# The squares of five pre-norms added to one pair of tiles on VectorE, so that TensorE sums two tiles instead of five

## The chip, the cores and the metric

The kernel runs on one core of one Trainium2 chip. The metric is the device time of one launch in microseconds (us), as the median of three runs. The times are compared kernel against kernel; the profile is of one further execution.

## The reference, cut to what matters

Two stacks of two layers each are applied to x of 256 tokens and 1024 channels, all in float32. Each layer of the first stack ("first block") is a pre-norm, a mixing part with three branches, an output projection with a norm of its own ("post-norm"), a sum with x, then the same around a feed-forward part. Each layer of the second stack ("second block") has a pre-norm before the mixing part and one before the feed-forward part. All these norms are root-mean-square norms over the 1024 channels:

```
xn = x * rsqrt(mean(x * x, channels) + eps) * g      # eps = 1e-6
```

With two layers a block there are eight such pre-norms: four in the first block and four in the second.

## The kernel before, in words

Channels lie on the 128 partitions, so that x is eight tiles of 128 channels by 256 tokens (`KD` = 8, `T` = 256), and the mean over channels is a sum over tiles and partitions. A column of sums over partitions is made on TensorE, by a product with a matrix of ones in plain float32 (`sumsq`, L599).

Nearly all of the work is products of weights and activations. Each float32 factor is split into two float32r parts (`hi`, `lo`), and a product is three float32r products. The weights come as a stream of 512 KB chunks of eight 128x128 blocks: a load to `wraw`, a rounding on ScalarE to `whi`, a subtraction on VectorE to `wlo` (`Weights.ensure`, L311; four buffers each). A chunk feeds 24 products of 256 columns. After four of the norms the first chunk of each of the first two products goes to TensorE as plain float32, against the tile `yw`.

The first two products after a pre-norm take x before it is scaled per token (tiles `yh`, `yl`), and their results are scaled on the way out of the accumulator (`dfr`). So the scale `r` of a token is needed only when those two products are done. By the third product, `whole` (L676) must have made the scaled x as `hh` and `hl`.

`post_norm` (L736) is where this change acts in four cases. It takes the unscaled result `zg` of an output projection and makes u = s * x + zg by pairs of tiles on VectorE; for each pair `feed` (L651) writes `yh` on ScalarE and `yl` on VectorE, and then sends the pair to `sumsq`: a square on ScalarE into a tile `sqt` (three buffers, one of which `yw` holds for a time), and an addition to the first pair's tile on VectorE, for as many pairs as `last` allows. At `last` the two halves of the sum are added too ("the fold"), and the result and the later tiles go to TensorE one by one. `end_norm` (L662) makes `r` from the sum in two steps on VectorE, with a square root on ScalarE and a reciprocal on VectorE.

`start_norm` (L640) sets `last` by its argument `folded`, which is 4 unless the caller says otherwise. Callers that say nothing are `run` (the first pre-norm, whose x is just being loaded) and `post_norm` (four pre-norms). `residual` (L1057) passes 6 for the three other pre-norms that have sums in their own products. `out_proj` (L774) calls `start_sum` itself with 6 and `hold`.

The order on each engine is fixed when the program is built: a planner simulates the program with costs of its own, takes the instructions in the order in which the program wrote them unless one isn't ready by its simulation, and so writes a queue for each engine. `issue_after` and `urgent` tie some instructions to come behind others; the weights after a norm of a feed-forward part have a higher priority (`W.first`). Steps of work beside the products (branches, attention) are woven in by `side` (L475), which keeps two counters, `pe` and `dve`, of estimated ns, and holds such steps back while `dve` is over `pe + SLACK` (4000).

Of the kernel before, what the change touches and what calls it, by code (L numbers as in the profile page):

```python
# [46 lines left out]
# norms after which the first chunks of weights and what they meet go unsplit  # L47
WHOLE = (1, 2, 3, 4)
# tiles of a product that ends a chain, the last ones apart
COLUMNS = ((0, 2), (2, 2), (4, 2), (6, 1), (7, 1))  # L50
# gates and products of the branches, in their order
# [8 lines left out]
def ffn_up(arr, l):  # L60
    """Gate and value tiles side by side; the first two products take four tiles."""
    t = [[_cols(i * P, P), _cols(FF + i * P, P)] for i in range(KF)]
    return [(arr, (l,), "B", KD, c) for c in [t[0] + t[1], t[2] + t[3]] + t[4:]]


def plan():
    """The weights in the order in which the tensor engine takes them: (array, index, kind,
    k tiles, columns), kind "B" by column tiles of 128 and "A" by rows of 512."""
    jobs = []

    def seg(arr, idx, nk, off, n, step=256):
        for i in range(0, n, step):
            jobs.append((arr, idx, "B", nk, [_cols(off + i + j, P) for j in range(0, step, P)]))

    def last_singly(arr, idx, nk):
        seg(arr, idx, nk, 0, D - 256)
        seg(arr, idx, nk, D - 256, 256, P)

    for l in range(DEPTH):
        seg("w_in", (l,), KD, OFF1["cfb"], 512, 512)  # L80
        seg("w_in", (l,), KD, OFF1["cfa"], 512, 512)
        for s, n in (("q", 256), ("k", 256)):
            seg("w_in", (l,), KD, OFF1[s], n)
        jobs.append(("w_in", (l,), "A", KD, _cols(OFF1["v"], 512)))
        for s, n in (("scc", 512), ("scx", 512), ("scb", 512), ("g", 512)):
            seg("w_in", (l,), KD, OFF1[s], n)
        for what, b in BRANCHES1:
            if what == "g":
                seg("w_in", (l,), KD, OFF1["gate"] + b * D, D)
            else:  # L90
                seg(("w_ret_out", "w_sc_out", "w_cf_out")[b], (l,), 4, 0, D)
        last_singly("w_o", (l,), KD)
        jobs += ffn_up("w_up", l)
        last_singly("w_down", (l,), KF)
    for l in range(DEPTH):
        w = "w_in_2"
        misc = np.full(P, -1)
        misc[:64] = _cols(OFF2["ik"], 64)
        misc[64:72] = _cols(OFF2["mif"], 8)
        misc[72:76] = _cols(OFF2["iw"], 4)  # L100
        jobs.append((w, (l,), "B", KD, [_cols(OFF2[s] + j, P) for s in ("iq", "ckv") for j in (0, P)]))
        seg(w, (l,), KD, OFF2["mqk"], 512, 512)
        jobs.append((w, (l,), "B", KD, [misc]))
        seg(w, (l,), KD, OFF2["mqk"] + 512, 512)
        jobs.append((w, (l,), "A", KD, _cols(OFF2["mv"], 512)))
        seg(w, (l,), KD, OFF2["mo"], 512)
        seg(w, (l,), KD, OFF2["dq"], 512)
        seg(w, (l,), KD, OFF2["dk"], 512)
        jobs.append((w, (l,), "A", KD, _cols(OFF2["dv"], 512)))
        seg("dsa_w_kv_up_2", (l,), 2, 0, 512)  # L110
        jobs.append(("dsa_w_kv_up_2", (l,), "A", 2, _cols(512, 512)))
        seg(w, (l,), KD, OFF2["sq"], 512)
        for what, b in BRANCHES2:
            if what == "g":
                seg(w, (l,), KD, OFF2["gate"] + b * D, D)
            else:
                seg("w_branch_2", (l, b), 4, 0, D)
        seg("w_out_2", (l,), KD, 0, D)
        jobs += ffn_up("w_gate_up_2", l)
        if l + 1 < DEPTH:  # L120
            seg("w_down_2", (l,), KF, 0, D)
        else:
            last_singly("w_down_2", (l,), KF)
    return jobs
# [48 lines left out]
def pack_params(inputs=None):  # L173
    """Per-channel parameters, channels on partitions: (offsets, array)."""
# [38 lines left out]
def make_consts():  # L213
    """Tables that depend on shapes alone: (offsets, array [128, n])."""
# [56 lines left out]
def whole_chunks():  # L271
    """The chunks that go to the tensor engine as float32, unsplit."""
    out, n, i = set(), 0, 0
    for _, _, kind, nk, cols in plan():
        if kind == "B" and len(cols) == 4:
            if i // 2 in WHOLE:
                out.add(n // CB)
            i += 1
        n += nk * (len(cols) if kind == "B" else 4)
    return out  # L280


class Weights:
    """The stream of weights: loads ahead, then each chunk as the sum of two float32r parts."""
# [13 lines left out]
    def cuts(self, c):  # L298
        """The first chunk comes in halves."""
        return [slice(0, CW // 2), slice(CW // 2, CW)] if c == 0 else [slice(0, CW)]  # L300
# [43 lines left out]
class Gen:  # L344
# [102 lines left out]
    def split(self, hi, lo, src):  # L447
        """src as the sum of its float32r rounding and of the exact rest."""
# [3 lines left out]
    def behind(self, engine):  # L452
        """What is traced here is issued after the engine's last urgent instruction."""
# [21 lines left out]
    def side(self):  # L475
        """Steps of the tasks beside the products, as far as the vector engine keeps up."""
# [13 lines left out]
    def job(self, evac, mov, needs=(), scale=None, last=False, spare=None):  # L490
        """The next product of the plan. mov(k) gives the two parts of the activations' tile k;
        scale, per token, is for activations that were not normalised yet; spare gives tiles."""
# [3 lines left out]
        if kind == "B":  # L496
            n = len(cols)
            accs = [self.acc() for _ in range(-(-n // 2))]
            if self.idle is not None:
                # only to keep the tensor engine's clock up while it waits  # L500
# [4 lines left out]
            for k in range(nk):  # L505
                xs = mov(k)
                for t in range(n):
# [4 lines left out]
                    # a start clears the marks of its whole bank: the first product of a bank has it  # L512
# [32 lines left out]
    def swap(self, out, src):  # L545
        """src with the halves of each 64 channels exchanged"""
# [3 lines left out]
    def rows(self, r):  # L550
        # r in DRAM, from where a row goes to many partitions
# [4 lines left out]
    def spread(self, out, row):  # L556
        """a row on all the partitions of out"""
        self.nc.sync.dma_start(out, row.to_broadcast(list(out.shape)))

# [31 lines left out]
    def rstd(self, pool, ps, scale, name):  # L591
        """1 / sqrt(scale * ps + eps)"""
# [6 lines left out]
    def sumsq(self, out, last, hold):  # L599
        """Over channels, on every partition: the sum of the squares of the eight tiles, which it  # L600
        takes by pairs, the last two also one by one (send). The first ones are added up before.
        With hold the tensor engine gets them together at the end."""
        ps = self.sp()[:, :T]
        n, todo = 0, []
        while n < KD:
# [14 lines left out]
            if n == last:  # L620
# [19 lines left out]
    def start_norm(self, g, l, folded=4):  # L640
        """Takes x by pairs of tiles (feed) for a norm whose scale per token comes last."""
# [20 lines left out]
    def end_norm(self, sd=None):  # L662
        """What the first products take, with their scale, and what the others take."""
# [38 lines left out]
    def branches(self, order, bufs, pool, mov, gate_load, needs, ys, done):  # L702
        """The sum over branches of gate * (branch output times its matrix), as two parts. A gate
        sigmoid(z) comes as tanh(z / 2), its double less 1."""
# [31 lines left out]
    def post_norm(self, zg, sums, gpre, l):  # L736
        """x += normalised zg; then the next norm's input. With s the root mean square of z, what
        the norm sees is u = s * x + zg, s times the new x."""
# [23 lines left out]
    def unscale(self, sd):  # L762
        """x out of u"""
# [10 lines left out]
    def out_proj(self, mov, g, l):  # L774
        """Four products whose columns are scaled by g, with the sum of their squares."""
# [11 lines left out]
    def first_mix(self, l, norm):  # L787
        dmov, rs, whole, mov = norm
        nc = self.nc
        with ExitStack() as st:  # L790
# [6 lines left out]
            def new_y(b):  # L797
                """Buffers for a branch's output, once those of the one before last are free."""
# [13 lines left out]
            # conformer convolution  # L812
# [65 lines left out]
            # retention  # L878
# [44 lines left out]
            # short convolution  # L923
# [133 lines left out]
    def residual(self, mov, gpre, l):  # L1057
        """x += four products; then the next norm's input."""
# [17 lines left out]
    def second_mix(self, l, norm):  # L1076
        dmov, rs, whole, mov = norm
        nc = self.nc
        with ExitStack() as st:
# [11 lines left out]
            def new_y(b):  # L1091
                """Buffers for a branch's output, once those of the one before last are free."""
# [14 lines left out]
            def rope(o):  # L1107
                """Rotates two tiles in place."""
# [6 lines left out]
            # indexer  # L1115
# [63 lines left out]
            # key/value rank  # L1179
# [33 lines left out]
            def q_task(sqs, dst, rq):  # L1213
                """rotation of the queries, and their scale per token and head"""
# [39 lines left out]
            # mLSTM queries and keys  # L1254
# [29 lines left out]
            # mLSTM gates  # L1284
# [102 lines left out]
            # attention with a softmax: sets of (queries, keys) of 64 channels  # L1387
            def softmax_group(q, k, rq, t, grp, bias, p, sums):
                """p = exp(scores - max) for the queries of tile t, sums its row sums. A group is
                sets in the same half of the partitions, one a tile."""  # L1390
# [22 lines left out]
            def transposed(p):  # L1413
                """p by keys: for each set its blocks of keys"""
# [18 lines left out]
            def ahead(q, k, rq, t, bias):  # L1433
                """The groups of tile t with their softmax, one group ahead."""
# [49 lines left out]
            def diff(l=l):  # L1484
                init = 0.8 - 0.6 * math.exp(-0.3 * l)
                for t in range(2):
                    yt = tl([P, 512], "yt", tag="yt", bufs=3)
                    for (half, tiles), p, sums in ahead(dq, dk, rq_d, t, None):
# [5 lines left out]
                        # both maps in one, up to the first one's sums  # L1494
# [44 lines left out]
            # differential attention  # L1539
# [22 lines left out]
            # sparse attention: keys and values out of the rank  # L1562
# [72 lines left out]
```

## Time and profile before

| what | value |
|---|---|
| time, median of 3 runs | 1789.97 us (1788.31 to 1790.07) |
| profiled execution: span from first to last instruction | 1789.1 us |
| TensorE busy | 1777.4 us of the span (99%) |
| VectorE busy | 1363.0 us (76%) |
| ScalarE busy | 1111.0 us (62%) |

For the profiled execution the page gives the span alone, and no time around it; the span is 0.9 us under the median of the runs. Busy time is the share in which an instruction of that engine was under way. Matmuls overlap each other, so the distance between their starts says more than the duration of one. A plain float32 product of 256 columns stands in the trace as two records, a float32r product as one.

### The profile page before, as it was taken

The page shows a single profiled execution, that of the slowest core. Times are in us where ns is not written, and L with a number is a line of the kernel's source. Part 1 is how long each engine was busy: PE and PEld are TensorE (multiplying, and loading weights), DVE is VectorE, ACT ScalarE, POOL GpSimd, SP SyncE. Part 2 cuts the span into 40 slices and gives each one's busy share as a digit, 9 for nine tenths or more (in the row PEclk, how much of TensorE's full clock was granted, in tenths as well). Part 3 has the DMA queues.
Part 4 walks back from the last instruction along what each step waited for, and adds up shares of the span by engine and source line. Part 5 has one row for each costly group of instructions (what it writes and reads, how often), then busy time and mean ns, then how long its engine had stood idle before and what let it go on. Part 6 is the DMA issues. An engine that isn't in the chain of part 4 may idle for free.

```text
span 1789.1 us, 35765 instructions
## 1 busy us (share of the span) xinstructions
PE 1777.4 (99%) x14462; PEld 1729.2 (97%) x14462; DVE 1363.0 (76%) x2082; ACT 1111.0 (62%) x1787; POOL 70.2 (4%) x144
## 2 busy tenths in 40 slices
PE   8999999999999999999999999999999999999999
PEld 8999999999999999999998999999999999999999
DVE  8988679865999769884887877865569887677553
ACT  7575468755666567765576666654457666655542
POOL 0000000000000000000022100000000310000000
PEclk9999999999999999999999999999999999999999
DMA  7555546554655546555465644565555664356663
GB/s 265 191 171 179 187 154 200 188 187 164 210 168 188 177 138 204 189 189 188 137 195 177 201 142 139 168 207 194 189 186 180 199 201 139 124 177 200 193 196 132
DMA packets 94648, 322.52 MB, mean 180 GB/s; under 512 B 12257, under 2 KB 16913, under 8 KB 94482
## 3 DMA queue, kind: packets, MB, share of 16 engines
q1 hardware_dynamic: 91010, 314.15, 53.9%
q0 software_dynamic: 3328, 6.09, 1.1%
q8 instruction: 113, 1.85, 0.4%
q14 instruction: 53, 0.43, 0.1%
q10 hardware_dynamic: 144, 0.00, 0.0%
HBM read 312.80 MB, written 1.10 MB: 175 GB/s over the span
## 4 chain that ended last, share of the span: by engine, by line
PE 97%; DVE 1%; DMA 1%; issue 0%; ACT 0%; POOL 0%; SPq 0%; DVEq 0%; ACTq 0%; POOLq 0%
PE acc L403 90%; PE sp L403 6%; PE sp L408 1%; DMA tmp<-dq 0%; DMA Wm<-rows 0%; DMA x<-x 0%; DVE wlo L415 0%; DVE sc L1167 0%; DVE x L415 0%; DVE m L1166 0%; DVE yw L420 0%; ACT sd L445 0%; DVE dq L415 0%; ACT whi L326 0%; POOL tmp L548 0%
## 5 line engine op out<-in xcount | busy, mean ns | idle before, releaser
L326 ACT ACTIVATE whi<-wraw 128x1024 fp32r<-128x1024 f32 (+1 forms) x575 | 606.7, 1057 | 535.9 <-PE acc L403 367.8
L415 DVE TENSOR_TENSOR wlo<-wraw,whi 128x1024 fp32r<-128x1024 f32 (+1 forms) x575 | 699.0, 1220 | 282.9 <-ACT whi L326 281.3
L403 PE MATMUL acc<-hh,whi 128*128 128x256 f32 x2832 | 791.4, 280 | 0.0
L403 PE MATMUL acc<-hl,whi 128*128 128x256 f32 x2832 | 790.8, 280 | 0.0
L403 PE MATMUL acc<-hh,wlo 128*128 128x256 f32 x2832 | 789.9, 280 | 0.0
L403 PEld LDWEIGHTS acc<-hh,whi 128*128 128x128 f32 x2832 | 531.0, 188 | 5.5 <-issue 3.7
L403 PEld LDWEIGHTS acc<-hl,whi 128*128 128x128 f32 x2832 | 531.7, 188 | 1.9 <-issue 1.2
L403 PEld LDWEIGHTS acc<-hh,wlo 128*128 128x128 f32 x2832 | 531.4, 188 | 1.1 <-issue 0.8
L403 PE MATMUL acc<-yh,whi 128*128 128x256 f32 x1280 | 269.7, 284 | 6.2 <-ACT whi L326 6.2
L403 PE MATMUL acc<-yh,wlo 128*128 128x256 f32 x832 | 231.3, 283 | 0.0
L403 PEld LDWEIGHTS acc<-yh,whi 128*128 128x128 f32 x1280 | 210.5, 190 | 7.1 <-ACT whi L326 6.2
L403 PE MATMUL acc<-fh,wlo 128*128 128x256 f32 x704 | 196.0, 278 | 0.0
L403 PE MATMUL acc<-fl,whi 128*128 128x256 f32 x704 | 195.6, 278 | 0.0
L403 PE MATMUL acc<-fh,whi 128*128 128x256 f32 x704 | 195.5, 278 | 0.0
L403 PEld LDWEIGHTS acc<-yh,wlo 128*128 128x128 f32 x832 | 155.8, 189 | 0.4
L403 PEld LDWEIGHTS acc<-fh,wlo 128*128 128x128 f32 x704 | 132.3, 188 | 0.0
L403 PEld LDWEIGHTS acc<-fl,whi 128*128 128x128 f32 x704 | 132.2, 188 | 0.0
L403 PEld LDWEIGHTS acc<-fh,whi 128*128 128x128 f32 x704 | 132.0, 188 | 0.0
L403 PE MATMUL acc<-yl,whi 128*128 128x256 f32 x384 | 108.2, 282 | 0.0
L403 PEld LDWEIGHTS acc<-yl,whi 128*128 128x128 f32 x384 | 72.1, 188 | 0.2
L445 ACT ACT_TABLE_LOAD x50 | 64.2, 1283 | 5.5 <-DVE Wm L426 3.0
L420 DVE SCALAR_TENSOR_TENSOR up<-z,prm,up 128x254 f32<-128x254 f32 (+1 forms) x128 | 55.3, 479 | 0.0
(282 smaller groups left out, 1815.2 us busy)
## 6 DMA issues: line engine op xcount, KB each, us to landing
wraw<-stream SPq DMA_DIRECT2D x581, 512.0 KB, 3.6
kr<-rows SPq DMA_DIRECT2D x32, 64.0 KB, 3.0
dec<-decay SPq DMA_DIRECT2D x2, 768.0 KB, 4.3
x<-x SPq DMA_DIRECT2D x4, 256.0 KB, 6.3
rf<-rows SPq DMA_DIRECT2D x8, 128.0 KB, 3.5
tmp<-dq POOLq DMA_DIRECT2D x16, 64.0 KB, 3.8
Wm<-rows SPq DMA_DIRECT2D x8, 128.0 KB, 3.6
tmp<-dk POOLq DMA_DIRECT2D x16, 64.0 KB, 3.9
```

Source lines behind the costliest of these rows:

```text
L326: nc.scalar.activation(h[:, s], r[:, s], AF.Copy)
L403: return self.nc.tensor.matmul(out, lhsT, rhs, start=start, stop=stop, **kw)
L408: return self.nc.tensor.transpose(out, in_, self.c("ident")[:k, :k])
L415: self.recent = self.nc.vector.tensor_tensor(out=out, in0=a, in1=b, op=op)
L420: return self.nc.vector.scalar_tensor_tensor(out, a, s, b, op0=op0, op1=op1)
L445: return self.nc.scalar.activation(out, in_, f, **kw)
```

## The change

`start_norm` takes all eight tiles as its default. In `sumsq`, when `last` is all eight tiles, the fold of the two halves is left out, and the two halves of the running sum go to TensorE as two products. Callers that pass 6 are as before. All other lines of the diff remove comments.

```
     def sumsq(self, out, last, hold):
...
             n += m
-            if n == last:
+            if n == last == KD:
+                todo += [acc[:, :T], acc[:, T:]]
+            elif n == last:
                 self.tt(acc[:, :T], acc[:, :T], acc[:, T:], OP.add)
                 todo.append(acc[:, :T])
             elif n > last:
...
-    def start_norm(self, g, l, folded=4):
+    def start_norm(self, g, l, folded=KD):
```

## Rows read from the trace of the kernel before

**Rows 1.** The page, part 1: busy us (share of the span) xinstructions.
```profile
PE 1777.4 (99%) x14462; PEld 1729.2 (97%) x14462; DVE 1363.0 (76%) x2082; ACT 1111.0 (62%) x1787; POOL 70.2 (4%) x144
```

**Rows 2.** The page, part 4: the chain that ended last, by engine.
```profile
PE 97%; DVE 1%; DMA 1%; issue 0%; ACT 0%; POOL 0%; SPq 0%; DVEq 0%; ACTq 0%; POOLq 0%
```

**Rows 3.** Waits of TensorE: us in total, times, longest us.
```profile
PE acc L403 <- ACT whi L326: 6.2, 1, 6.2
PE acc L403 <- DVE yw L420: 1.0, 4, 0.3
PE sp L403 <- DVE Wm L420: 0.8, 1, 0.8
```

**Rows 4.** The chain in order of time: start us, us, what.
```profile
12.49 1.29 PE sp L403 x6
...
16.73 0.86 PE sp L403 x4
...
249.49 2.16 PE sp L403 x10
251.65 177.61 PE acc L403 x1508
...
442.45 2.16 PE sp L403 x10
...
866.66 2.16 PE sp L403 x10
```

**Rows 5.** Timeline of TensorE after the first post-norm: start us, us, instruction.
```profile
248.85 0.64 PE L403 MATMUL acc<-yh,whi 128*128 128x256 f32 x4
...
249.32 2.32 PE L403 MATMUL sp<-sqt,ones 128*128 128x256 f32 x10
...
265.14 0.28 PE L403 MATMUL acc<-hh,whi 128*128 128x256 f32 x1
265.26 0.28 PE L403 MATMUL acc<-hl,whi 128*128 128x256 f32 x1
```

**Rows 6.** Timeline of VectorE after the first post-norm.
```profile
244.45 0.68 DVE L415 TENSOR_TENSOR sqt<-sqt 128x512 f32<-128x512 f32 x1
...
245.05 0.48 DVE L420 SCALAR_TENSOR_TENSOR yh<-x,prm,yh 128x256 fp32r<-128x256 f32 x1
...
246.44 0.42 DVE L415 TENSOR_TENSOR sqt<-sqt 128x256 f32<-128x256 f32 x1
...
246.78 0.87 DVE L420 SCALAR_TENSOR_TENSOR yh<-x,prm,yh 128x256 fp32r<-128x256 f32 x2
...
247.58 2.35 DVE L415 TENSOR_TENSOR wlo<-wraw,whi 128x1024 fp32r<-128x1024 f32 x2
...
250.18 2.45 DVE L415 TENSOR_TENSOR wlo<-wraw,whi 128x1024 fp32r<-128x1024 f32 x2
...
252.56 0.42 DVE L420 SCALAR_TENSOR_TENSOR r<-sp,r 128x256 f32<-128x256 f32 x1
...
262.12 1.29 DVE L415 TENSOR_TENSOR hl<-yn,hh 128x512 fp32r<-128x512 f32 x2
```

**Rows 7.** Timeline of ScalarE after the first post-norm.
```profile
246.98 0.62 ACT L445 ACTIVATE sqt<-x 128x512 f32<-128x512 f32 x1
```

**Rows 8.** Timeline of VectorE after the second and the fourth post-norm.
```profile
440.99 4.85 DVE L415 TENSOR_TENSOR wlo<-wraw,whi 128x1024 fp32r<-128x1024 f32 x4
...
455.21 0.69 DVE L415 TENSOR_TENSOR hl<-yn,hh 128x512 fp32r<-128x512 f32 x1
...
865.08 3.50 DVE L415 TENSOR_TENSOR wlo<-wraw,whi 128x1024 fp32r<-128x1024 f32 x3
```

**Rows 9.** Timeline of TensorE, the second post-norm's third product.
```profile
458.23 0.28 PE L403 MATMUL acc<-hl,whi 128*128 128x256 f32 x1
```

**Rows 10.** Timeline of VectorE at the start of the kernel, with its idle time.
```profile
14.62 0.88 DVE L420 SCALAR_TENSOR_TENSOR yh<-x,g,yh 128x256 fp32r<-128x256 f32 x2 [0.69 <-ACT yh L445]
16.48 1.23 DVE L415 TENSOR_TENSOR wlo<-wraw,whi 128x1024 fp32r<-128x1024 f32 x1 [0.98 <-ACT whi L326]
```

**Rows 11.** Windows in the second block: us, busy us (x instructions) of each engine, clock, DMA.
```profile
930.00:940.00 10.00, 10.00 (x85) 9.71 (x83) 8.23 (x16) 9.37 (x12) 6.40 (x10) 1.00 0.63 189
...
950.00:960.00 10.00, 10.00 (x55) 8.53 (x55) 6.34 (x13) 4.79 (x6) 1.21 (x1) 1.00 0.52 161
960.00:970.00 10.00, 9.23 (x53) 7.62 (x52) 9.20 (x18) 8.55 (x16) 5.51 (x12) 1.00 0.63 206
```

More of the change, by code (lines that the diff above doesn't have):

```diff
@@ L619, in sumsq @@
             n += m
-            if n == last:
+            if n == last == KD:
+                todo += [acc[:, :T], acc[:, T:]]
+            elif n == last:
                 self.tt(acc[:, :T], acc[:, :T], acc[:, T:], OP.add)
@@ L638, in start_sum, with start_norm @@
         return g, out
-    def start_norm(self, g, l, folded=4):
+    def start_norm(self, g, l, folded=KD):
         parts = [self.xpool.tile([P, 4, T], F32R, name="yh", tag=tag, bufs=2)
```

## The prediction

> **What bounds the kernel now.** I read the busy times first, then the chain that ended last, then the waits of TensorE, and last the queues around each norm. TensorE is busy for 99% of the span [rows 1]. That alone proves little, since a matmul's duration overlaps the next one's. The chain is the better witness: 97% of it runs over TensorE [rows 2], and the waits put down to it are 6.2 us for the first weights and 1.8 us in all the rest [rows 3]. In the chain the work after a norm goes on without a break: 1508 products in 177.61 us, one per 0.1178 us [rows 4]. So in most stages time is what TensorE's queue holds, and a product taken out of it gives back its distance to the next start, if nothing that TensorE reads comes later.
>
> The change touches five places, all before 870 us: the kernel's start and the four post-norms. In each, the five sums stand in that queue as ten records of plain float32. In the post-norms the ten run back to back for 2.16 us [rows 4]; the third post-norm, between those shown at 442 and 866 us, has the same figure. At the start they come as six and four, 1.29 and 0.86 us [rows 4].
>
> **The change part by part.**
>
> *Removed from TensorE.* Three products in each of five norms. Ten records take 2.16 us, so one takes 0.216, and a product of two records 0.43 us. Four records stay: 0.86 us. Saved per norm 2.16 - 0.86 = 1.30 us, in five norms 6.5 us. This is the only term that can make the kernel faster directly.
>
> *Added to VectorE.* Per norm two additions of 128x512 (third and fourth pair) come in, and one fold of 128x256 goes. The addition at 244.45 is followed by the next start at 245.05, so it costs 0.60 us of the queue; the fold at 246.44 is followed at 246.78, 0.34 us [rows 6]. The sum is 2 x 0.60 - 0.34 = 0.86 us a norm, 4.3 us in all. On an engine that is busy 76% [rows 1] this is not on the chain by itself. It costs nothing if covered by two things: weights converted ahead, and the time between the sums and the third product. Without cover it costs up to 0.86 us a norm.
>
> *The third pair's addition* takes the place of the fold, so the last pair's two `yl` steps start 0.60 - 0.34 = 0.26 us later. These tiles are needed only by the chunk behind the one that begins at 248.85, so at least 24 products, 2.8 us, later [rows 5]; they are done at 247.65 today. Cost nothing.
>
> *The last addition* is new in the way of the sum. The last square ends at 246.98 + 0.62 = 247.60 [rows 7]. If the addition runs at once, behind the `yl` pair that ends at 247.65 [rows 6] plus the shift of 0.26, it is done at about 248.6, and TensorE, which today comes to the sums at 249.3 [rows 5], doesn't wait. Two sums then end at about 250.2, before today's 251.65. If it runs behind the two weight subtractions of 247.58, it ends at 249.93 + 0.60 = 250.5. The planner writes TensorE's queue from the same simulated times as VectorE's, so I expect that it then puts the sums later, behind more products that are ready. The row today shows the pattern: four products of the next chunk first, then the sums, 1.7 us after the last square. I take no wait; the other end is a rival below.
>
> *The scale r.* Its second step ran at 252.56, behind four subtractions, though the sums had ended at 251.65 [rows 4, 6]. So VectorE's queue set it, not TensorE, and shorter sums don't bring it forward. With 0.86 us more in that queue it comes 0 to 0.86 us later; I take 0.86. What is late next is `hl`: its first tile is done at 262.12 + 0.69 = 262.8, and TensorE first reads it at 265.26 [rows 5, 6], a margin of 2.4 us. In the second post-norm it is 455.21 + 0.69 = 455.9 against 458.23, 2.3 us [rows 8, 9]. The change uses up 1.30 (TensorE comes sooner) + 0.86 (VectorE comes later) = 2.16 us of it. It holds, with 0.1 to 0.2 us left. The other tiles of `hl` are read six products apart, 0.7 us, while each takes 0.60 us or, with a weight subtraction between, more; that may cost some tenths.
>
> *Buffers.* The running sum holds its `sqt` tile until the end, as it does now until the sums; the other squares take turns, as the wait of the third square on the second's addition already has it. Cost nothing. DMA issues don't move.
>
> *The start.* VectorE has idle gaps of 0.69 and 0.98 us around the last pair [rows 10], so the added 0.86 us fits, and I count the full 1.30 us.
>
> *The sum.* 6.5 us removed. For tenths lost at `hl` in four norms I take 0.1 to 0.2 each, 0.5 us. Net 6.0 us of the span: 1789.1 - 6.0 = 1783.1. The median of the runs is 0.9 above the span, so 1784.0. After the last norm touched, everything should merely start earlier: the stretch about 930 to 967 us, where the chain leaves TensorE, begins behind a product.
>
> **The rivals.** A measurement of this kernel can tell about 0.2%, 3.6 us, from no change: under 1786.4 is faster, over 1793.5 slower.
>
> *VectorE becomes the bound after each norm.* The margin before `hl` is 2.3 us and 2.16 of it goes. If the planner's new order puts one more weight subtraction (1.2 us, half of the 2.35 us pair [rows 6]) ahead of `hl`, TensorE waits about 1.1 us at the third product, in four norms 4.4 us. What is left is 6.5 - 4.4 = 2.1, or nothing if it is worse: 1787.5 to 1790. For it speaks how closely the sums agree; against it, that four chunks of weights are held converted, which gives the planner room to let `hl` pass.
>
> *The sums stand at the head of TensorE's queue and wait for the last addition behind weight subtractions.* In the first post-norm behind all four, 250.18 + 2.45 + 0.60 = 253.2 against 249.3: 3.9 us. In the second behind four, 440.99 + 4.85 + 0.60 = 446.4 against 442.45: 4.0 [rows 4, 8]. In the fourth behind three, 865.08 + 3.50 + 0.60 = 869.2 against 866.66: 2.5. Taking 2.5 to 4.0 in four norms, 10 to 16 us are lost against 6.5 won: 1793.5 to 1799.5. It decides from 1.6 us a norm on (no gain), and from 2.5 us on it is measurably slower. For it speaks that these subtractions are ready at just that moment, and that after the feed-forward norms they have priority; against it, that in all four post-norms today the sums are placed with their squares long done, and TensorE shows no wait for them [rows 3].
> The Trainium skill, in Perfetto Trace Analysis, section Optimizing Scalar/DVE Operations, says that instructions of an engine which isn't saturated but leaves gaps on others may be broken up so that work ends sooner; the last addition does the reverse, one of 512 columns ahead of both sums. By that advice halves would let the first sum start earlier; no row of the kernel before shows a gap there, so it only adds weight to this rival.
>
> *The order of other work shifts.* The kernel's counters move by 3 x 256 x 1.68 = 1290 ns on `pe` and by 2 x 602 - 336 = 868 ns on `dve` in each of these norms, 2.2 us against a slack of 4. So branch work can start one step later, and the queues of the whole stage can come out otherwise. Where the chain leaves TensorE, it issues 108 instructions in 20 us where 85 in 10 us is its rate just before [rows 11]: 62 fewer at 0.1178, at most 7.3 us of waiting that the busy time hides. I let half of that go either way, 3.6 us around the forecast: 1780.4 to 1787.6, and a little beyond if several stages move.
>
> That the change does nothing is out: five norms use the default, and their ten records are in the chain.
>
> **How the numbers follow.** The forecast as worked out (1783 to 1786) has 0.60. VectorE as bound has 0.18, all of it within 0.2%. Sums that wait have 0.08, slower. A shifted order has 0.14: 0.05 faster, 0.05 same, 0.04 slower. So faster 0.65, same 0.23, slower 0.12. The likeliest is 1784.0. The range goes down to 1780.5, the better end of a shifted order, and up to 1790.0, the end of VectorE as bound; the sums that wait and the worst of the shifted order are left out, about 0.15.
>
> **What the profile of the changed kernel would show.** Right: four records of sums, 0.86 us, in each of five norms; no TensorE wait there; the third product of each norm 1.3 us closer to the first; the sums of the fourth post-norm (at 866.66 us today) some 4.5 to 5 us earlier, being behind four of the five savings; additions of 512 in the place of folds. Wrong: a TensorE wait for VectorE at the sums (second rival) or at the first `hh`/`hl` product (first rival); or stages far from the norms that changed in length (third). The forecast fails if a norm loses more than half of its 1.3 us.

## The result, and the profile after

The changed kernel takes 1802.3 us (median of 4 runs: 1794.87, 1801.99, 1802.6, 1803.5) against 1790.02 us before (4 runs). The ratio is 1.006, with a 95% interval from 1.0048 to 1.0072: slower by 0.6%, where 1784.0 us, 0.3% less, was forecast. The profiled execution is the one of 1794.87 us, with a span of 1793.2 us. A second one, taken for the experiments below (label e8_again), has 1802.84 us and a span of 1801.1. The two differ most by the pace of the products in one stage, which the last section shows. The waits below are in both; behind the first two waits the granted clock fell less in the first profile than in the second.

The page of the changed kernel, parts 1 and 4 (busy time by engine; the chain that ended last, by engine):

```profile
PE 1768.0 (99%) x14432; PEld 1719.4 (96%) x14432; DVE 1366.9 (76%) x2087; ACT 1114.1 (62%) x1787; POOL 68.9 (4%) x144
...
PE 96%; DVE 2%; ACT 0%; issue 0%; DMA 0%; ACTq 0%; DVEq 0%; SPq 0%
```

TensorE has exactly 30 records less than in [rows 1]: five norms, three products, two records each. VectorE has five instructions more: two additions in and one fold out, five times. So the change did what it says, and TensorE is no less the busiest engine. But busy time doesn't show the new waits; its list of waits does (us in total, times, longest):

```profile
PE acc L403 <- DVE hl L415: 10.7, 4, 4.1
PE acc L403 <- ACT whi L326: 8.1, 3, 6.2
PE acc L403 <- ACT hh L445: 1.7, 2, 1.2
PE acc L403 <- DVE yw L420: 1.0, 4, 0.3
```

Beside [rows 3], two entries are new: `hl`, four times, and `hh`; `whi` has two waits more, of 1.2 and 0.6 us, in and behind the fourth post-norm. The waits for `hl` and `hh` are at the third product after a post-norm. TensorE in the first of them, in order of time (in brackets: idle time before, and what ended it):

```profile
251.97 1.03 PE L403 MATMUL sp<-sqt,ones 128*128 128x256 f32 x4
...
262.23 0.50 PE L403 MATMUL acc<-hh,whi 128*128 128x256 f32 x2 [0.50 <-ACT hh L445]
266.83 0.58 PE L403 MATMUL acc<-hl,whi 128*128 128x256 f32 x1 [4.10 <-DVE hl L415]
```

This norm's first products start at 237.07, in the kernel before at 239.01. Counted from there, the sums come at 14.9 us where they came at 10.3 [rows 5], TensorE is ready for the third product at 24.7 (it starts it at 25.2, after 0.5 us for `hh`) where it was at 26.1, and it reads the first `hl` at 29.8 where it read it at 26.25. VectorE in the same norm:

```profile
245.90 2.35 DVE L415 TENSOR_TENSOR wlo<-wraw,whi 128x1024 fp32r<-128x1024 f32 x2
248.17 0.41 DVE L420 SCALAR_TENSOR_TENSOR r<-sd 128x256 f32<-128x256 f32 x1
248.51 0.68 DVE L415 TENSOR_TENSOR sqt<-sqt 128x512 f32<-128x512 f32 x1
249.11 2.35 DVE L415 TENSOR_TENSOR wlo<-wraw,whi 128x1024 fp32r<-128x1024 f32 x2
...
253.04 0.42 DVE L420 SCALAR_TENSOR_TENSOR r<-sp,r 128x256 f32<-128x256 f32 x1
...
257.89 3.25 DVE L420 SCALAR_TENSOR_TENSOR yn<-x,prm,r 128x256 f32<-128x256 f32 x8
261.05 1.22 DVE L415 TENSOR_TENSOR wlo<-wraw,whi 128x1024 fp32r<-128x1024 f32 x1
262.19 1.26 DVE L420 SCALAR_TENSOR_TENSOR up<-dfr,prm,up 128x254 f32<-128x254 f32 x3
263.37 0.68 DVE L415 TENSOR_TENSOR dfr<-acc,r 128x512 f32<-128x512 f32 x1
...
266.10 1.28 DVE L415 TENSOR_TENSOR hl<-yn,hh 128x512 fp32r<-128x512 f32 x2
```

Two things are to be seen. The last addition stands at 248.51, behind two weight subtractions, 2.85 us after its square ended (245.66), and the second step of `r` comes at 253.04: 16.0 us after the first product, where it was 13.55 [rows 6]. And behind `r` the order has turned. In the kernel before, two `dfr` steps of the first product's evacuation ran ahead of the first `hl` (262.12 [rows 6]), and the rest behind it; ScalarE made `hh` before its own eight steps of that evacuation. VectorE and ScalarE of the kernel before:

```profile
259.79 1.29 DVE L415 TENSOR_TENSOR dfr<-acc,r 128x512 f32<-128x512 f32 x2
...
265.67 1.27 DVE L420 SCALAR_TENSOR_TENSOR up<-dfr,prm,up 128x254 f32<-128x254 f32 x3
...
258.18 1.14 ACT L445 ACTIVATE hh<-yn 128x512 fp32r<-128x512 f32 x2
```

In the changed kernel all four `dfr` and four `up` steps of VectorE run ahead of `hl`, and ScalarE takes its eight steps before `hh`:

```profile
261.57 1.65 ACT L445 ACTIVATE hh<-yn 128x512 fp32r<-128x512 f32 x3
```

So `hh` starts 24.5 us after the first product instead of 19.2, and `hl` 29.0 us after it instead of 23.1 [rows 6]. From `r` to `hl` there are 13.1 us where there were 9.6.

The third effect comes behind the wait. Windows of TensorE in the second profile, where the first post-norm's wait ends at 267.06 and the third's at 700.83 (us, busy us (x instructions), granted clock, DMA):

```profile
256.00:260.00 4.00, 4.00 (x36) 1.00 0.70 263
...
264.00:268.00 4.00, 0.94 (x4) 0.76 0.39 124
268.00:272.00 4.00, 4.00 (x21) 0.50 0.53 185
272.00:276.00 4.00, 4.00 (x32) 0.89 0.13 53
...
700.00:704.00 4.00, 3.17 (x15) 0.50 0.41 135
704.00:708.00 4.00, 4.00 (x26) 0.70 0.37 133
```

TensorE stood still for 4.1 us, the granted clock fell to 0.50, that is from 2.4 to 1.2 GHz, and 21 products were issued in four us instead of 36.

Stage by stage, in us, as differences of starts read from the timelines ("first" is a post-norm's first product with `yw`, "third" the first product that reads `hl`):

| stage | before | after, 1801.1 us | difference | after, 1793.2 us |
|---|---|---|---|---|
| start to first, norm 1 | 239.01 | 237.29 | -1.7 | 237.07 |
| first to third, norm 1 | 26.25 | 29.77 | +3.5 | 29.76 |
| third, norm 1, to first, norm 2 | 166.83 | 169.43 | +2.6 | 168.23 |
| first to third, norm 2 | 26.14 | 27.15 | +1.0 | 27.20 |
| third, norm 2, to first, norm 3 | 204.88 | 206.66 | +1.8 | 205.13 |
| first to third, norm 3 | 26.25 | 30.53 | +4.3 | 30.49 |
| third, norm 3, to first, norm 4 | 166.83 | 169.30 | +2.5 | 163.27 |
| first to third, norm 4 | 27.11 | 26.91 | -0.2 | 27.56 |
| third, norm 4, to the end | 905.80 | 904.06 | -1.7 | 904.49 |

The first to third stages lose 8.6 us in spite of the 1.3 us saved in each, the three long stages behind a wait lose 6.9 us more, and 3.5 us are won at the two ends: +12.0 us in the second profile.

### The profile page after: what moved, and what is told of

It reads as the page before. It is cut to its first block, busy times and chain, and to the rows that moved or that the text cites. A ratio compares the mean times of both kernels' runs of the same rounds, so it can differ in the third digit from the quotient of the medians.

```text
span 1793.2 us, 35727 instructions
## 1 busy us (share of the span) xinstructions
PE 1768.0 (99%) x14432; PEld 1719.4 (96%) x14432; DVE 1366.9 (76%) x2087; ACT 1114.1 (62%) x1787; POOL 68.9 (4%) x144
## 4 chain that ended last, share of the span: by engine, by line
PE 96%; DVE 2%; ACT 0%; issue 0%; DMA 0%; ACTq 0%; DVEq 0%; SPq 0%
PE acc L403 90%; PE sp L403 6%; PE sp L408 1%; DVE wlo L415 0%; DVE x L415 0%; DVE yn L420 0%; DVE dfr L415 0%; DMA x<-x 0%; DMA wraw<-stream 0%; ACT whi L326 0%; DVE up L420 0%; DVE yw L420 0%; DVE hl L415 0%; DVE yh L420 0%; ACT sd L445 0%
## 5 line engine op out<-in xcount | busy, mean ns | idle before, releaser
L445 ACT ACTIVATE tap<-glu,prm 128x256 f32<-128x256 f32 x120 | 50.8, 496 | 6.2 <-DVE glu L415 5.3
```

The source lines that it names most:

```text
L445: return self.nc.scalar.activation(out, in_, f, **kw)
```

## Experiments

The theory at first: the sum ends later, so that at the time `r` is there the first product's results are there too; the planner then lets their evacuation go ahead of `hh` and `hl`; the order is the cost. The first rival: the later `r` and the 0.86 us more on VectorE are enough by themselves. The second: it is the shorter queue of TensorE. The third: nothing was saved at all. None of them leaves out a part of the computation; e2 adds a step that changes no value, e11 products that nothing reads. In the text below, "r" and "hl" are the starts on VectorE of the second step of `r` and of the first `hl`, "third" is the first product that reads `hl`, all as means over the four post-norms, in us from the first product, out of the profiled execution. Before: r 13.8, hl 22.9, third 26.4. Changed (second profile): r 16.2, hl 27.9, third 28.6.

**e1_start_only.** All eight squares on VectorE only in the norm at the start.

```
-    def start_norm(self, g, l, folded=KD):
+    def start_norm(self, g, l, folded=4):
...
-        self.start_norm("norm_mix_pre", 0)
+        self.start_norm("norm_mix_pre", 0, KD)
```

> One of the five places alone: all eight squares are added on VectorE only in the norm at the kernel's start; the four post-norms keep five sums. Theory (in the post-norms r comes later while the first product ends sooner, so the evacuation of the first product goes ahead of hh and hl on ScalarE and VectorE, and the third product waits for hl): nothing of that here, about 1.3 to 1.9 us gained, 1788 to 1789, no wait for hl. Rival (the saved sums give nothing back anywhere, TensorE's queue isn't what sets the time): 1790 and no change at the start either.

Measured: 1789.05 us against 1790.05, ratio 0.9995 (0.9986 to 1.0005). By the timing alone it can't be told from no change. The profile tells it: the first post-norm's first product starts at 237.61 instead of 239.01, 1.4 us sooner, there is no wait for `hl`, and the stages behind are as long as before (26.25, 166.83, 26.25, 204.88). A single start scatters by some tenths: over the profiles it is 239.0 to 239.7 in the three kernels with five sums there and 237.0 to 237.7 in those with two. The products taken out do give back what they took, where nothing stands in the way.

**e2_max.** The kernel before, its five sums kept, with one VectorE step of 128x512 between the last squares and their sums (added to the kernel before; it acts in the norm at the start too).

```
+            if n == KD - 2 and last == 4:
+                self.tt(sq[:, :m * T], sq[:, :m * T], sq[:, :m * T], OP.max)
             if n == 4:
                 self.act(self.warm, sq[:, 0:1], AF.Sqrt)
```

> The kernel before with its five sums, but the last pair's squares pass through VectorE first (maximum of the tile with itself, 128x512, which leaves them as they are). Theory (the late finish of the sums turns the order round): waits of several us for hl at the third product, without the 6.5 us saved: 1797 to 1808. Rival (it is the shorter queue of TensorE, which leaves VectorE less time, and not the later finish of the sums): 1790 to 1792 and waits under 1 us a norm.

Measured: 1793.33 us, ratio 1.0009 (0.9996 to 1.0023); the runs lie at 1787 (three) and at 1793 to 1795 (six). r 15.6, hl 26.2, third 27.3. Between the two expectations. The later finish of the sums makes `r` 1.9 us and `hl` 3.2 us later with no product taken away, so a shorter queue is not the cause of that. But the waits for `hl` are 3.4 us in all and not 10.5, because TensorE comes to the third product later, at 25.7 to 26.7 us. The loss needs both: `hl` late and TensorE early.

**e3_whole_first.** The changed kernel, with the making of `hh` and `hl` under a higher priority of the planner.

```
             for i in range(KD // 2 + 1):
+              with self.tc.high_priority():
                 if i < KD // 2:
                     y = spare("yn")
```

> The changed kernel, with the making of hh and hl given priority in the planner over the evacuation of the first product. The sums end as late as in the changed kernel. Theory (the order is what costs): hl early enough, waits under 1 us a norm, 1783 to 1787. Rival (the later r and the 0.86 us more on VectorE are enough by themselves): waits of over 2 us a norm remain, 1793 or more.

Measured: 1797.52 us, ratio 1.0045 (1.003 to 1.006). r 16.3, hl 26.1, third 27.6; waits for `hl` 9.1 us. From `r` to `hl` there are 9.8 us on average, against 11.6 in the changed kernel and 9.2 before: the order is nearly as it was. That was not enough. My theory, that the order is the cost, falls here: the rival is closer to it. VectorE of the first post-norm:

```profile
248.90 0.69 DVE L415 TENSOR_TENSOR sqt<-sqt 128x512 f32<-128x512 f32 x1
...
254.28 0.42 DVE L420 SCALAR_TENSOR_TENSOR r<-sp,r 128x256 f32<-128x256 f32 x1
...
264.56 0.69 DVE L415 TENSOR_TENSOR hl<-yn,hh 128x512 fp32r<-128x512 f32 x1
265.16 0.69 DVE L415 TENSOR_TENSOR dfr<-acc,r 128x512 f32<-128x512 f32 x1
265.76 1.29 DVE L415 TENSOR_TENSOR hl<-yn,hh 128x512 fp32r<-128x512 f32 x2
```

`hl` is now ahead of the second `dfr` pair, but `r` stands where the late sum puts it.

**e4_urgent.** The changed kernel, with the weight subtractions tied to come behind the last addition.

```
-                self.tt(acc[:, :m * T], acc[:, :m * T], sq[:, :m * T], OP.add)
+                ins = self.tt(acc[:, :m * T], acc[:, :m * T], sq[:, :m * T], OP.add)
+                if n + m == last == KD:
+                    self.urgent["dve"] = ins
```

> The changed kernel, with the weight subtractions tied to come behind the last addition, so that the sums can end some 2 us earlier; the making of hh and hl is not given priority. Theory (order is what costs): the evacuation still goes ahead of hl where both are ready, so waits of 1 to 3 us a norm remain, 1788 to 1798. Rival (the place of the last addition behind weight subtractions is the whole cost): waits gone, 1783 to 1785.

Measured: 1792.79 us, ratio 1.0006 (0.9995 to 1.0018); runs at 1787 (four) and 1792.6 to 1794.6 (six). r 14.3, hl 25.9, third 26.9; waits for `hl` 6.2 us. Theory as expected: the sums are back at 10.3 us and `r` is nearly in time, but from `r` to `hl` there are still 11.6 us. The last addition in the first post-norm:

```profile
246.12 0.68 DVE L415 TENSOR_TENSOR sqt<-sqt 128x512 f32<-128x512 f32 x1
246.73 2.35 DVE L415 TENSOR_TENSOR wlo<-wraw,whi 128x1024 fp32r<-128x1024 f32 x2
```

So the delay of `hl` has two parts of like size. Over the four norms, in the first profile of the changed kernel, `hl` starts 20.4 us later than before: 10.5 us of it lie ahead of `r`, 9.8 between `r` and `hl`. e4 leaves 2.2 of the one and 9.6 of the other, e3 leaves 10.0 and 2.5.

**e5_both.** Both edits together.

> The changed kernel with both earlier edits together: the weight subtractions come behind the last addition, and the making of hh and hl has priority. By the first four runs the delay of hl has two parts, about 2.5 us a norm from the later scale r and about 2.5 from the turned order; the one edit took away most of the first, the other of the second. Theory (the two parts add): hl about 1 us a norm later than in the kernel before, waits at the third product under 0.7 us a norm, no fall of the granted clock, 1784 to 1786. Rival (either part alone is enough to spend the margin, since TensorE comes 1.3 us sooner and 0.86 us more lies on VectorE): waits of 2 us a norm remain, 1790 to 1794.

Measured: 1789.96 us, ratio 0.9983 (0.9968 to 0.9998), with seven of twelve runs at 1790 to 1792 and five at 1777 to 1786. r 14.3, hl 24.9, third 26.7. The runs at 1790 to 1792 win nothing: the rival was closer. In the profiled execution (1783.11 us) 6.2 us are the shorter pace in one stage (last section), and the four first to third stages together take 0.9 us more than in the kernel before. In the first post-norm TensorE now comes at 24.3 us and waits:

```profile
261.75 0.39 PE L403 MATMUL acc<-hh,whi 128*128 128x256 f32 x2
264.47 0.39 PE L403 MATMUL acc<-hl,whi 128*128 128x256 f32 x1 [2.34 <-DVE hl L415]
```

VectorE in this norm:

```profile
262.00 0.68 DVE L415 TENSOR_TENSOR hl<-yn,hh 128x512 fp32r<-128x512 f32 x1
...
263.73 0.68 DVE L415 TENSOR_TENSOR hl<-yn,hh 128x512 fp32r<-128x512 f32 x1
```

The first `hl` was done at 262.68, the second at 264.41: the first read was released by the second. That is 1.7 us of this wait. In the first and third post-norm the read was released by the second `hl` step in e3, e5, e6 and e9, by the third in e10, and by the first in the changed kernel, e2, e4 and e11; in the second post-norm it was the first in all of these. So in those two norms it goes with the priority for `hh` and `hl`; the rows don't show why.

**e6_six_whole_first.** Six tiles added and folded, three products, no addition behind the last square (`folded=6` as the default), with the priority of e3.

> Another split: six tiles are added on VectorE and folded, three products in place of five or two, so no addition stands behind the last square; the making of hh and hl has priority. Theory: 4 records fewer a norm, 0.86 us in five norms, 4.3 us gained less tenths of waiting, 1785.5 to 1787.5. Rival (any more work on VectorE in the norm spends the margin): waits of 1 to 2 us a norm, 1789 to 1793.

Measured: 1795.26 us, ratio 1.003 (1.0019 to 1.0041), worse than either expectation. In the first and third post-norm the sums come at 14.3 us, as late as in the changed kernel, though no addition stands behind the last square: here the fold stands behind two weight subtractions. In the other two they come at 10.3. VectorE of the first:

```profile
247.55 2.35 DVE L415 TENSOR_TENSOR wlo<-wraw,whi 128x1024 fp32r<-128x1024 f32 x2
249.82 0.41 DVE L415 TENSOR_TENSOR sqt<-sqt 128x256 f32<-128x256 f32 x1
```

So which VectorE step ends up behind them doesn't matter, only that one does.

**e7_before_whole_first.** The kernel before with the priority of e3 alone.

> The kernel before with priority for hh and hl alone, five sums as they were. Theory (there hl had a margin of 2.3 us and the order was right already): no change, 1789 to 1791. Rival (that priority is a gain of its own, which would explain what the other runs with it gain): 1787 or less.

Measured: 1789.95 us, ratio 0.9985 (0.9973 to 0.9996), with six runs at 1790 to 1791 and four at 1783 to 1784. Its profiled run has a span of 1789.3, the same stages as before within 0.25 us but for the start (239.66) and the end (0.6 us shorter), and no wait for `hl`. The priority alone gains nothing that the profile shows. The four shorter runs may be the other pace; none of them was profiled, and none of the 71 runs of the kernel before lies under 1787.17, so it stays open whether the priority makes that pace more frequent.

**e8_again.** The changed kernel once more, no edit.

> The changed kernel once more, for a second profile. Its runs lay at 1794.9 and at 1802 to 1803.5; the profiled one was the 1794.9, and in it the products after the third post-norm's wait ran at 0.1133 us each, against 0.1178 in the kernel before. Theory (the 7 us between the runs are this pace, over the some 1400 products of that stage): if the time is near 1802, the stage from the third post-norm's wait to the fourth post-norm takes 167 to 170 us and not 163, at 0.1178 a product. Rival (the runs differ by longer waits or a longer fall of the clock): pace 0.1133 again, and waits or clock in other stages make the difference.

Measured: 1802.84 us, with the stage from the third post-norm's wait to the fourth norm at 169.30 us (the table above). The 7 us between the runs are the pace there, as the theory had it: 6.0 of 7.9 us between the spans lie in this stage. The first two long stages are 1.2 and 1.5 us longer, with a deeper fall of the clock (0.50 against 0.75 at 268 to 272 us, 0.57 against 1.00 at 464 to 468), and the fourth post-norm and the end are 1.0 us shorter.

**e9_r_early.** As e5, and from the third weight subtraction on they come behind the second step of `r`.

```
-            self.stt(r, out[0], 1.0 / D, r, OP.mult, OP.add)
+            self.r2 = self.stt(r, out[0], 1.0 / D, r, OP.mult, OP.add)
+            self.r2n = 2
...
-                    with self.g.behind("dve"):
+                    with self.g.behind("dve"), self.g.after_r():
...
+    def after_r(self):
+        if self.r2 is None or self.r2n > 0:
+            self.r2n -= 1
+            return nullcontext()
+        return self.tc.issue_after(self.r2.ins)
```

> As the fifth run (weight subtractions behind the last addition, priority for hh and hl), and from the third weight subtraction on they also come behind the second step of the scale r, which there stood behind four of them some 3 us after the sums had ended. Theory (hl's lateness against TensorE's earlier arrival is the whole loss): r's second step about 2 us earlier, hl no later after the first product than in the kernel before, waits under 0.5 us a norm, and at a pace of 0.118 us a product 1784 to 1786. Rival (the 0.86 us more on VectorE and the 1.3 us that TensorE comes sooner are too much for any order, so that the gain of a shorter queue is only turned into waiting): waits stay near 2 us a norm, 1789 to 1791 at that pace.

Measured: 1784.66 us against 1789.94, ratio 0.9975 (0.9965 to 0.9985): faster than both kernels. r 12.1, hl 23.9, third 25.3; waits for `hl` 1.7 us in all. VectorE and then TensorE in the first post-norm:

```profile
248.74 0.42 DVE L421 SCALAR_TENSOR_TENSOR r<-sd 128x256 f32<-128x256 f32 x1
249.27 0.42 DVE L421 SCALAR_TENSOR_TENSOR r<-sp,r 128x256 f32<-128x256 f32 x1
249.61 2.35 DVE L416 TENSOR_TENSOR wlo<-wraw,whi 128x1024 fp32r<-128x1024 f32 x2
...
261.25 1.88 DVE L416 TENSOR_TENSOR hl<-yn,hh 128x512 fp32r<-128x512 f32 x3
```

```profile
261.36 0.39 PE L404 MATMUL acc<-hh,whi 128*128 128x256 f32 x2
262.58 0.39 PE L404 MATMUL acc<-hl,whi 128*128 128x256 f32 x1 [0.83 <-DVE hl L416]
```

`r` is 2.2 us earlier than in e5, as expected. `hl` is 1.0 us earlier than there, but still 1.0 us later than in the kernel before (23.9 against 22.9), which was not expected. In the first post-norm TensorE comes to the third product at 24.3 where it came at 26.1; the margin is just spent, with waits of 0.83 us in the first and third post-norm and none to speak of in the others. With so little waiting the shorter queue is worth about what it was forecast to be: eight of nine runs lie at 1784.2 to 1786.5. The profiled execution is the ninth, with the shorter pace in one stage (last section). Apart from that stage, its start is 2.0 us and its four first to third stages together 4.7 us shorter than in the kernel before; in these four the products behind the sums ran at the shorter pace too, some 0.5 us a norm where TensorE did not wait.

**e10_reciprocal_early.** As e9, but from the third on the subtractions come behind the reciprocal (`self.r2` is the reciprocal).

> As the ninth run, but from the third on the weight subtractions come behind the reciprocal that ends the making of r. Theory: r earlier by another 1 us, but three weight subtractions then stand ready ahead of hh and hl, so the waits are no smaller than in the ninth run; 1784 to 1787. Rival (only the time of r counts): 0.5 to 1 us a norm better than the ninth run.

Measured: 1792.92 us, ratio 1.0015 (1.0006 to 1.0024). In the first post-norm the reciprocal starts 1.2 us sooner than in e9 counted in the span, 1.7 us counted from the first product, but three subtractions stand ready behind it. `hl` starts at 24.5 on average (e9: 23.9), and in the first and third post-norm the read waits for the third `hl` step; waits for `hl` are 6.4 us. The direction is the theory's, the size is worse than expected:

```profile
250.69 1.75 DVE L435 RECIPROCAL r<-r 128x256 f32<-128x256 f32 x1 [0.48 <-ACT r L446]
252.36 3.43 DVE L416 TENSOR_TENSOR wlo<-wraw,whi 128x1024 fp32r<-128x1024 f32 x3
255.70 3.25 DVE L421 SCALAR_TENSOR_TENSOR yn<-x,prm,r 128x256 f32<-128x256 f32 x8
```

**e11_fillers.** The changed kernel with five products of ones on TensorE ahead of the third product.

```
...
+            self.since += 1
+            if self.since == 3:
+                with self.tc.issue_after(self.prev_mm.ins):
+                    for _ in range(5):
+                        self.mm(accs[0][:, :T], self.ones[:, :P], self.ones[:, :T])
...
```

> The changed kernel with five products of ones with ones (2.2 us, results overwritten) put on TensorE between the second and the third product after each post-norm, in the place of part of the wait. In the second profile of the changed kernel, the granted clock fell to about 0.5 for 4 to 8 us behind the waits of the first three post-norms, and the stages that follow took 2.6, 1.8 and 2.5 us longer than in the kernel before. Theory (that length is the clock's fall after the idle time): the clock stays at or near 1.0, those stages come back to within 0.5 us of the kernel before, and the time goes from 1802 to 1795 to 1797. Rival (the stages are longer because the weights or activations stay late): no change, 1800 to 1804.

Measured: 1800.81 us, ratio 1.0065 (1.0052 to 1.0078), 2 us under the second run of the changed kernel and not 5 to 7. By stages the theory holds where the clock stayed up; there the long stages are those of the kernel before: 204.86 us behind the second and 166.83 behind the third post-norm, against 206.66 and 169.30. Behind the first the clock still fell, and it is 168.14. Windows as above, behind the first and the third post-norm's wait (TensorE, clock, DMA):

```profile
268.00:272.00 4.00, 3.77 (x20) 0.60 0.39 131
...
700.00:704.00 4.00, 4.00 (x37) 1.00 0.50 179
```

That is 5.6 us won. The fillers themselves cost 2.0 us in the stages from first to third, most of it in the fourth post-norm, where there was little to fill, and the ends of the kernel lost another 0.9.

## Why the prediction was wrong

**Right:** the removed term. Ten records became four (0.86 us) in each of five norms; e1 gives 1.4 us for the start where 1.30 was counted, and TensorE is ready for the first post-norm's third product 1.1 to 1.5 us sooner in the two profiles. VectorE's additions are as costed (0.60 us from start to start). TensorE doesn't wait at the sums: the planner put them behind other products, as said, and the rival in which they wait at the head of the queue did not happen. Two small readings were off, and neither made the miss: each run's time is 1.7 us above its own span (1794.87 and 1793.2), not 0.9, and one VectorE step of `hl` makes two tiles, which serve twelve products of the third product, 1.4 us, not six.

**The step that failed** is "The scale r": "With 0.86 us more in that queue it comes 0 to 0.86 us later; I take 0.86." It came 2.4 to 2.9 us later in the first profile, because the last addition was placed behind two weight subtractions and the sums then 4.1 to 4.6 us later in TensorE's queue. I had seen that place, worked out that the addition would end at 250.5, and then charged nothing for it, since I asked only whether TensorE would wait for the sums, not who waits for their result. e2 shows that a later end of the sums alone delays `r` (by 1.9 us), and e4 that with the addition in front `r` is only 0.55 us late and the time 1792.79 us instead of 1802.3; e9 puts `r` in front too.

**The step behind it**, "It holds, with 0.1 to 0.2 us left", took for granted that `hl` follows `r` at the same distance. That distance grew by 0.8 to 3.8 us, since the evacuation of the first product went ahead of `hh` and `hl`; that the planner found it ready at the same time is inferred, not shown. e3 gives most of that part back, but neither e3 nor e4 alone gains anything. In e5, with both, `hl` is still 1.9 us late and read one step later than needed in two norms, and most of its runs gain nothing; in e9, with `hl` 1.0 us late, the gain is there.

**The rival that happened** was the first, VectorE as the bound after each norm, with 0.18. Its place was right, its price wrong: 1.1 us a norm was taken for one subtraction more, and 0.2 to 4.1 us were measured for `hl` alone where TensorE waited.

**Not in the prediction at all:** that a wait of some us costs again what the clock does behind it. In the second profile the three long stages are 6.9 us longer, more than the whole saving; e11 gives back 5.6 of it where the clock stays up. The Trainium skill, in TensorE: Matmul & The Clock Gate, section Part 1: The HAM clock gate, says that the engine's clock is halved unless the engine has been busy; the trace agrees with 0.50 behind the waits of 4.1 us in the second profile.

**Open:** the stage behind the fourth post-norm, 905.80 us before and 904.06 to 904.49 after, takes 903.9 to 906.9 us over all the profiles, and what moves it was not found; nor why the first read of `hl` is released by a later step in the kernels with priority for it.

## What to carry to other kernels

When an edit makes a result come later, follow that result to the engine that reads it last, not only to the next one, and compare the whole delay with the margin there; a margin of 2.3 us that both sides eat into is gone sooner than a queue is shortened. In a kernel whose order comes from a planner, a step that is ready a little later can change places with several others, so look at what else is ready by then, and tie the few steps that the chain needs. The saving of this change is real, but it shows only with the last addition, the scale and `hl` held in front (e9, 0.9975). These orders were not run with the five sums of the kernel before; its list of waits [rows 3] has none for `hl` that they could win back.

## What the runs showed of the hardware

The same kind of products runs at one of two paces, at a granted clock of 1.00 in both, and the pace can change at a wait or at the plain float32 sums of a norm. In the kernel before, the products behind the first post-norm take 0.1178 us each [rows 4]. Behind another norm's sums, with no wait there, they take 0.1133 us in the same execution (length by count):

```profile
1150.37 166.84 PE acc L403 x1472
```

In e9 the products take 0.118 us ahead of the first post-norm's sums and 0.1133 behind them, without a wait between. The chain of the changed kernel's first profile has the same stretch of 1390 records twice, behind the first and behind the third post-norm's wait:

```profile
266.83 165.39 PE acc L403 x1390
...
697.88 160.44 PE acc L403 x1390
```

The length of the wait doesn't decide it, since both stretches begin behind a wait of 4.1 us with a fall of the clock. In e9 the shorter one is the first, and the clock doesn't fall in either:

```profile
262.58 158.08 PE acc L404 x1390
...
678.23 164.19 PE acc L404 x1390
```

These are 6.1 us apart, or 0.1137 and 0.1181 us a product (length by count). In the second profile of the changed kernel both stretches take the longer pace, 166.60 and 166.47 us. In e4 the stage from the third post-norm's third product to the fourth norm takes 160.92 us where it takes 166.83 before, at the shorter pace. In these stretches a pace, once taken, holds to the end. The two profiles of the changed kernel show that this can set two runs of one kernel 6 us apart. The two groups of runs in e2, e4, e5 and e7 fit it, but of each only one execution was profiled; e9's profiled execution is the one of its nine that lies 6 us below the others. The kernel before showed only the longer pace behind its post-norms in its profile, and its runs show no second group. What sets the pace was not tried, and no row names it.

The clock doesn't follow the length of a wait alone either. Behind waits of 2.83 us (e6) and 2.96 us (e3), both in the third post-norm, it stayed at 1.00; behind 1.79 us (e2, first post-norm) and 2.26 us (second profile of the changed kernel, second post-norm) it fell to 0.50. At the longer pace, the stages behind the first and third post-norm take 168.1 to 169.4 us where it fell, and 166.8 to 167.8 where it stayed up; the longest of these have further waits in them.
